# A hybrid decoder layer in split float32: all gate and up panels in rows, on rows that are not normed, with the tokens' factor spread by loads

## The chip, the cores and the metric

The kernel runs on one core of one Trainium2 chip. The metric is the device time of one execution in microseconds (us); the median of several executions counts. TensorE (PE) multiplies matrices into PSUM, VectorE (DVE) and ScalarE (ACT) work elementwise, GpSimd (POOL) does a few small things, and SyncE (SP) issues the DMA transfers. A granted clock of 1.0 is full speed for TensorE.

## The reference

One layer on 256 tokens of width 1024, everything in float32:

```python
h    = rms_norm(x, ln1_g)
proj = h @ w_in                     # q, k, v, z, xbc, dt, gate_a, gate_b
y_a  = moba_attention(norm(q), norm(k), v) @ w_o_attn
y_b  = mamba2_mixer(z, xbc, dt, ...) @ w_o_ssm
x    = x + (sigmoid(gate_a) * y_a + sigmoid(gate_b) * y_b) @ w_out
h2   = rms_norm(x, ln2_g)           # x * rsqrt(mean(x * x) + eps) * ln2_g
g_ff, u_ff = split(h2 @ w_gate_up)  # 1024 x 5632
x    = x + (silu(g_ff) * u_ff) @ w_down
h3   = rms_norm(x, ln3_g)
x    = x + (p @ w_ple_proj) * sigmoid(h3 @ w_ple_gate)
```

An RMS norm is a factor for each token (one over the root of its mean square) times a gain for each feature. The factor of a token can be taken out of a matrix product and applied to the sums; the gain cannot.

## The kernel before

**Split numbers.** Each product is made in parts to keep float32's precision: a number is the sum of a rounded high part and the low rest. For weights the high part `wh` is made by ScalarE, the low part `wl` by VectorE (`split_w`, L257). Of the four products of parts, three are made (high by high, high by low, low by high).

**Weights.** All weights stream from DRAM once. `next_chunk` (L318) loads a chunk of four k-tiles (512 rows) by 512 columns as two tiles of 512 KB, by SP, and splits each. There are five raw buffers, four of `wh` and six of `wl` (L252), so that loads and splits run ahead of TensorE until buffers are short.

**Two forms of a panel.** A panel is 512 columns of a product over all 1024 rows of the weights, in two chunks.
- `Panel` (L334) is over tokens: the activations are the stationary operand, the weights are streamed. For each k-tile and each half of the tokens there are three products of 512 columns. The result has tokens on partitions, so a token's factor is a scale for each partition, but features that go into the next product must be transposed afterwards.
- `Rows` (L379) has the weights stationary and streams the activations' rows, high and low part side by side (2 x 256 columns). For each k-tile and each tile of 128 features there is one product of 512 columns with `wh` and one of 256 with `wl`. The halves of the sums are added afterwards on VectorE. The result has features on partitions, as the next product needs it, and the tokens run along the free axis, so a token's factor would have to be a row of 256 that stands on all partitions.

`Rows.add_all` (L386) makes blocks of two k-tiles for one feature tile (two products with `wh`, two with `wl`). In the first chunk the blocks are sorted by feature tile, in the second by k-tiles. After the last block of a feature tile `after` takes its sums.

**Order of the work.** TensorE's order is written out: the main products follow each other, and a `Filler` (L78) puts small tasks (transposes, the scan's and attention's products) between them once a planned time has come; `LAG` (L68) holds the waiting times, in planned ns. `fill.drain` runs tasks until some condition holds. On the other engines a planner orders instructions by priority: weights ("w") first, then evacuations ("ev"), then background ("bg").

**The tokens' factor, first norm.** `x_stats` (L414) computes `rstd1` with tokens on partitions. `norm_task` (L437) makes a row of it on all partitions: ScalarE scales the identity by it, TensorE multiplies that by a matrix of ones (L444), ScalarE copies the result out twice. Then the eight row tiles are multiplied by it and split.

**The tokens' factor, second norm.** `Residual.take` (L1053) adds the residual, starts the transposes and splits into rows that carry the gain but not the factor (`split_t`, L990), and computes `rstd2`. The first two of the eleven gate and up panels are over tokens (`pair`, L1068), on these rows without the factor; `evac_gu` (L1095) scales the sums by `rstd2`, and `ff_task` (L1105) transposes and splits the result. Beside them `norm2` (L1120) spreads `rstd2` by ones as above (L1130) and makes eight normed rows: high and low part added, multiplied by the factor, split again (L1138 to L1142). The other nine panels are in rows, on the normed rows. For each, `rows_gu` (L1145) copies a feature tile's sums (ScalarE), adds their halves (L1152), and `end` (L1156) makes silu(g) * u, its high and its low part.

Of the kernel before, what the change touches and what calls it, by code (L numbers as in the profile page):

```python
# [36 lines left out]
    ('q', 1, 512),  # L37
    ('k', 0, 1024),
    ('k', 1, 1536),
# [29 lines left out]
    "norm": 0, "norm.x": 7982, "norm.k": 5731, "dt": 3113, "dt.t": 1660, "dt.e": 891, "dt.low": 0,  # L69
    "dt.end": 5490, "xbc": 3857, "xbc.t": 2999, "xbc.end": 16627, "z": 0, "z.t": 3129, "z.end": 768,  # L70
    "qk": 15739, "qk.t": 6258, "qk.end": 0, "v": 1782, "cb": 3077, "rows": 0, "prep": 877, "seg": 102,
    "seg.next": 9127, "out": 8638, "out.xdt": 352, "out.end": 545, "off": 3241, "off.end": 51, "finish": 4321,
    "finish.ones": 8093, "sc": 1152, "sc.tr": 1416, "tr": 2000, "tr.val": 0, "val": 5094, "val.end": 1076,
    "m": 811, "res": 3010, "ff": 0, "ff.end": 500, "n2": 1163, "n2.rows": 2102, "n2.k": 0, "gu": 0,
# [34 lines left out]
def tile_layer(ctx: ExitStack, tc: tile.TileContext, head, xk, pt, vec, w_dt, w_big, w_dn2, w_pp, out):  # L109
# [15 lines left out]
    psb = ctx.enter_context(tc.tile_pool(name="psb", bufs=4, space=bass.MemoryType.PSUM))  # L125
    fill = Filler()
# [69 lines left out]
    with prio("w"):  # L196
        zero = nc.const_aps.tensor(0.0, (P, P), F32)
        pw = pb([512])
        for _ in range(7):
            nc.tensor.matmul(pw[:, :P], zero, zero, start=True, stop=True)  # L200
# [8 lines left out]
        ones_m = const.tile([P, P], F32, name="ones_m")  # L209
        nc.gpsimd.memset(ones_m, 1.0)  # L210
# [168 lines left out]
    class Rows:  # L379
# [6 lines left out]
        def add_all(self, acts, after):  # L386

            for c0 in (0, 4):
                parts = next_chunk()
                runs = [(k0, b) for k0 in (c0, c0 + 2) for b in range(4)]  # L390
                for k0, b in runs if c0 else sorted(runs, key=lambda r: r[1]):
                    cs = slice(b * P, b * P + P)
                    with prio("mm"):
                        for k in (k0, k0 + 1):
                            mm(self.ps[b], parts[k % 4][0][:, cs], acts[k], k == 0, False, main=True)
                        for k in (k0, k0 + 1):
                            mm(self.ps[b][:, :T], parts[k % 4][1][:, cs], acts[k][:, :T], False, k == 7, main=True)
                    fill.now += 52.0
                    fill.step()
                    if k0 == 6:  # L400
                        after(b, self.ps[b])
# [34 lines left out]

    def norm_task():  # L437
        yield fill.now + LAG["norm"]
        with prio("bg"):
            dg = s2([2, P])  # L440
            for tt in range(2):
                act(dg[:, tt], ident, scale=rstd1[:, tt : tt + 1])
            pr = pb([512])
            mm(pr[:, :T], ones_m, dg.rearrange("p a t -> p (a t)"), True, True)  # L444
            rbc = s2([2, T])
            for j in range(2):
                act(rbc[:, j], pr[:, :T])
# [24 lines left out]
    e1d = ctx.enter_context(tc.tile_pool(name="dram", bufs=1, space=bass.MemoryType.DRAM)).tile([32, P], F32, name="e1d")  # L472
# [517 lines left out]
    def split_t(toks, scale_cols, const_scale, acts, delay, tiles=None):  # L990

        th = s4([4, T], F32R)
        tl = s4([4, T], F32R)
        if tiles is not None:
            tiles.append((th, tl))
        yield fill.now + delay
        for jj in range(2):
            with prio("bg"):
# [8 lines left out]
                else:  # L1007
                    for j in range(2):
                        k = 2 * jj + j
                        act(th[:, k], pm[:, j], scale=scale_cols[k])  # L1010
                        stt(tl[:, k], pm[:, j], scale_cols[k], th[:, k].bitcast(F32), op0=ALU.mult, op1=ALU.subtract)
            yield fill.now
        acts.extend((th[:, k], tl[:, k]) for k in range(4))
# [32 lines left out]
    class Residual:  # L1046


        def __init__(self, base, vcol, dst_rstd):
            self.base, self.vcol, self.dst, self.acts, self.tiles = base, vcol, dst_rstd, [[], []], []  # L1050
            self.ss = const.tile([P, 2, 2], F32, name=nm("ss"))

        def take(self, n, pan):  # L1053
# [4 lines left out]
            fill.spawn(split_t([b[:, 0], b[:, 1]], [v[:, self.vcol + 4 * n + k : self.vcol + 4 * n + k + 1] for k in range(4)], None, self.acts[n], LAG["res"], self.tiles), 0)  # L1058
# [21 lines left out]
    res2 = Residual(xin, V_G2, rstd2)  # L1080
# [14 lines left out]
    def evac_gu(_, pan):  # L1095
        t = s2([2, T])
        with prio("ev"):
            for tt in range(2):
                r = rstd2[:, tt : tt + 1]
                act(t[:, tt], pan.ps[tt][:, :T], AF.Sigmoid, scale=r)  # L1100
                stt(t[:, tt], pan.ps[tt][:, :T], r, t[:, tt], op0=ALU.mult, op1=ALU.mult)
                stt(t[:, tt], pan.ps[tt][:, T:], r, t[:, tt], op0=ALU.mult, op1=ALU.mult)
        fill.spawn(ff_task(t), 0, LAG["ff"])

    def ff_task(t):  # L1105
        with prio("bg"):
            pm = pb([2, T])
            for tt in range(2):
                for j in range(2):
                    transpose(pm[:, j, tt * P : tt * P + P], t[:, tt, j * P : j * P + P])  # L1110
            f2 = s4([2, 2, T], F32R)
            fh, fl = f2[:, 0], f2[:, 1]
            act(fh, pm)
            nc.vector.tensor_sub(fl, pm, fh.bitcast(F32))
        yield fill.now + LAG["ff.end"]
        ff.extend((fh[:, j], fl[:, j]) for j in range(2))

    h2n = []

    def norm2():  # L1120

        yield fill.now + LAG["n2"]
        with prio("bg"):
            dg = s2([2, P])
            for tt in range(2):
                act(dg[:, tt], ident, scale=rstd2[:, tt : tt + 1])
        yield fill.now + LAG["n2.rows"]
        with prio("bg"):
            pr = pb([512])
            mm(pr[:, :T], ones_m, dg.rearrange("p a t -> p (a t)"), True, True)  # L1130
            rbc = s2([T])
            act(rbc, pr[:, :T])
        for k in range(0, 8, 2):
            yield fill.now + LAG["n2.k"]
            th, tl = (res2.tiles[k // 4][m][:, k % 4 : k % 4 + 2] for m in range(2))
            with prio("bg"):
                t = s2([2, T])
                nc.vector.tensor_add(t, th.bitcast(F32), tl.bitcast(F32))  # L1138
                nc.vector.tensor_tensor(t, t, rbc.unsqueeze(1).to_broadcast([P, 2, T]), op=ALU.mult)
                h = s4([2, 2, T], F32R)  # L1140
                act(h[:, :, 0], t)
                nc.vector.tensor_sub(h[:, :, 1], t, h[:, :, 0].bitcast(F32))  # L1142
            h2n.extend(h[:, j].rearrange("p a t -> p (a t)") for j in range(2))

    def rows_gu(i):  # L1145
        gu = s4([4, T])

        def after(b, ps):
            with prio("ev"):
                e = s2([512])  # L1150
                act(e, ps)
                nc.vector.tensor_add(gu[:, b], e[:, :T], e[:, T:])  # L1152
            if b == 3:
# [16 lines left out]

    fill.spawn(norm2(), 0)
    pair(res2.acts, evac_gu)
    h2 = res2.acts[0] + res2.acts[1]
    for i in range(2, 2):
        pan = Panel()
        for hf in range(2):
            pan.add(next_chunk(), h2[4 * hf : 4 * hf + 4], last=hf == 1)
        evac_gu(i, pan)
    fill.drain(lambda: len(h2n) == 8)
    for i in range(2, NFF):  # L1180
        Rows().add_all(h2n, rows_gu(i))
# [24 lines left out]
def _layout(i):  # L1206
# [30 lines left out]
    big += [chunks(gu, 512 * n, 4 * g, 4) for g in range(2) for n in range(2)]  # L1237
    for n in range(2, NFF):
# [39 lines left out]
```

## Time and profile before

| what | value |
|---|---|
| median of 3 runs | 584.73 us (584.73 to 586.01) |
| the profiled execution | 585.25 us |
| its span, first to last instruction | 583.5 us |
| TensorE, products: busy | 578.3 us, 99% |
| VectorE, ScalarE, GpSimd: busy | 457.7, 373.1, 47.4 us |
| moved by DMA | 104.97 MB, mean 180 GB/s |
| granted clock of TensorE | 1.000 |
| DMA queue q1: share of 16 engines' span | 52.9% |

The profile is of one execution. A row of the timeline is: start, length, engine, line, operation, out<-in, shape, count of merged instructions; in brackets the idle time before it and what ended it. All matrix products are issued by a helper at L170, the transposes by one at L192, ScalarE's activations by one at L151, so they are told apart by the names of the tiles: `g` are the sums of a panel over tokens, `gr` those of one in rows, `pb` those of a small task, `wh` and `wl` the weights' parts. Matrix products are pipelined and the length of one covers part of the next; the distance of two starts is what one costs.

### The profile page before, as it was taken

What the parts mean: (1) busy time and instruction counts of PE and PEld (TensorE: products, weight loads), DVE (VectorE), ACT (ScalarE), POOL (GpSimd) and SP (SyncE); (2) the same over time, 40 slices, a digit from 0 to 9 for tenths busy, and PEclk for the clock granted to TensorE, in tenths of its full rate; (3) what the DMA queues carried; (4) which work ended last, traced back from release to release, by engine and by line L of the source; (5) the groups of instructions that cost most, each with busy time, mean ns of one, the idle gap of its engine ahead of it and who ended that gap; (6) DMA issues with size and microseconds to landing.
All of it is one profiled execution on the core that took longest, in us unless ns stands there. A gap on an engine that the chain in (4) does not pass through costs nothing.

```text
span 583.5 us, 8612 instructions
## 1 busy us (share of the span) xinstructions
PE 578.3 (99%) x3119; PEld 490.9 (84%) x3119; DVE 457.7 (78%) x745; ACT 373.1 (64%) x582; POOL 47.4 (8%) x44
## 2 busy tenths in 40 slices
PE   9999999999999999999999999999999999999997
PEld 8888888888888888888888888888888888888886
DVE  5686889998998998998898765897777777546464
ACT  7874678676997668666644345766667567535452
POOL 2003100220000311151101000000000000000000
PEclk9999999999999999999999999999999999999999
DMA  8956455476345424435546575555546646565521
GB/s 314 372 188 223 149 182 189 168 194 225 118 154 181 145 79 140 145 111 181 181 144 198 202 258 176 179 181 192 183 163 206 205 153 208 198 202 181 184 71 72
DMA packets 33322, 104.97 MB, mean 180 GB/s; under 512 B 3616, under 2 KB 7040, under 8 KB 33280
## 3 DMA queue, kind: packets, MB, share of 16 engines
q1 hardware_dynamic: 32992, 104.16, 52.9%
q8 instruction: 24, 0.39, 0.3%
q10 hardware_dynamic: 288, 0.26, 0.2%
q14 instruction: 18, 0.15, 0.1%
HBM read 103.28 MB, written 1.06 MB: 179 GB/s over the span
## 4 chain that ended last, share of the span: by engine, by line
PE 99%; DMA 0%; ACT 0%; DVE 0%; issue 0%
PE g L170 52%; PE gr L170 36%; PE pb L170 7%; PE pb L192 3%; DMA x<-in_head 0%; ACT s L151 0%; DVE s L1199 0%; DVE s L1200 0%; ACT wh L151 0%
## 5 line engine op out<-in xcount | busy, mean ns | idle before, releaser
L260 DVE TENSOR_TENSOR wl<-raw,wh 128x1024 fp32r<-128x1024 f32 (+2 forms) x193 | 230.8, 1203 | 90.9 <-ACT wh L151 89.7
L170 PE MATMUL g<-wh,s 128*128 128x512 f32 (+1 forms) x900 | 282.5, 391 | 0.2 <-ACT wh L151 0.2
L151 ACT ACTIVATE wh<-raw 128x1024 fp32r<-128x1024 f32 (+2 forms) x193 | 198.4, 1037 | 131.6 <-PE g L170 81.5
L170 PEld LDWEIGHTS g<-wh,s 128*128 128x128 f32 x900 | 168.8, 189 | 34.7 <-issue 0.5
L170 PE MATMUL gr<-s,wh 128*128 128x512 f32 x608 | 193.5, 399 | 0.0
L170 PE MATMUL g<-wl,s 128*128 128x512 f32 (+1 forms) x450 | 173.3, 387 | 0.0
L170 PEld LDWEIGHTS gr<-s,wl 128*128 128x128 f32 x608 | 114.2, 188 | 26.9
L170 PE MATMUL gr<-s,wl 128*128 128x256 f32 x608 | 119.9, 278 | 0.0
L170 PEld LDWEIGHTS g<-wl,s 128*128 128x128 f32 x450 | 84.4, 188 | 16.4
L170 PEld LDWEIGHTS gr<-s,wh 128*128 128x128 f32 x608 | 93.5, 189 | 1.5 <-issue 0.5
L151 ACT ACTIVATE s<-s 128x512 f32<-128x512 f32 (+2 forms) x49 | 36.6, 747 | 25.4 <-DVE s L1161 15.6
L151 ACT ACTIVATE s<-gr 128x512 f32<-128x512 f32 x76 | 44.3, 592 | 4.2 <-PE gr L170 2.2
L711 POOL TENSOR_SCALAR_AFFINE_SELECT rr<-a_h 128x512 fp32r<-128x512 f32 x16 | 23.8, 1508 | 159.1 <-PE pb L170 118.6
L151 ACT ACTIVATE s<-pb 128x512 f32<-128x512 f32 (+3 forms) x50 | 24.0, 515 | 18.2 <-PE pb L170 12.5
L574 DVE SCALAR_TENSOR_TENSOR s<-s,vecs,s 128x255 f32<-128x255 f32 (+2 forms) x72 | 33.1, 500 | 0.1
L170 PE MATMUL pb<-s,s 128*64 128x128 f32 (+4 forms) x288 | 31.3, 302 | 0.0
L170 PEld LDWEIGHTS pb<-s,s 128*64 128x64 f32 (+1 forms) x288 | 24.7, 154 | 3.9 <-issue 1.2
L192 PE MATMUL pb<-ident,s 128*128 128x128 f32 x170 | 25.0, 273 | 0.0
L406 POOL TENSOR_TENSOR rstd<-tiny,mhalf 128x2 f32<-128x2 f32 x3 | 2.1, 707 | 261.9 <-DVE tiny L405 242.2
L192 PEld LDWEIGHTS pb<-ident,s 128*128 128x128 f32 x170 | 20.3, 141 | 3.0 <-DVE wl L260 0.4
L151 ACT ACTIVATE s<-s,vecs 128x256 f32<-128x256 f32 (+1 forms) x40 | 20.1, 556 | 0.1
L151 ACT ACTIVATE s<-s,tiny,fq 128x128 f32<-128x128 f32 (+1 forms) x32 | 17.1, 537 | 2.0 <-DVE tiny L856 2.0
(146 smaller groups left out, 341.6 us busy)
## 6 DMA issues: line engine op xcount, KB each, us to landing
raw<-in_w_big SPq DMA_DIRECT2D x176, 512.0 KB
raw<-in_head SPq DMA_DIRECT2D x4, 512.0 KB
s<-in_xk SPq DMA_DIRECT2D x4, 512.0 KB
raw<-in_head SPq DMA_DIRECT2D x7, 256.0 KB
e1c<-e1d SPq DMA_DIRECT2D x2, 512.0 KB
raw<-in_w_pp SPq DMA_DIRECT2D x2, 512.0 KB
raw<-in_w_dn SPq DMA_DIRECT2D x2, 512.0 KB
out<-s SPq DMA_DIRECT2D x3, 256.0 KB
```

Source lines behind the costliest of these rows:

```text
L151: return nc.scalar.activation(o, i, f, **kw)
L170: ins = nc.tensor.matmul(o, lhsT, rhs, start=start, stop=stop).ins
L192: queue(nc.tensor.transpose(o, i, ident[: i.shape[0], : i.shape[0]]).ins, False)
L260: nc.vector.tensor_sub(wl, raw, wh.bitcast(F32))
L406: nc.gpsimd.tensor_tensor(dst, t, mhalf[:, : ss.shape[-1]], op=ALU.pow)
L574: stt(cc[:, sft:], u[:, b, : T - sft], cw[3 - sft], cc[:, sft:], op0=ALU.mult, op1=ALU.add)
L711: nc.gpsimd.affine_select(r, bcast(a_h[:, c, h0 : h0 + 4].bitcast(F32), P), pattern=[[0, 4], [1, P]], compare_op=ALU.is_ge, fill=0.0, base ...
```

## The change

- `norm2`, `evac_gu` and `ff_task` go, and with them the two panels over tokens. All eleven gate and up panels are in rows.
- Their rows are those of `split_t`, with the gain and without the factor. `split_t` now writes high and low part of a k-tile side by side, as `Rows` streams them, when it is given a list `rows`.
- The factor is applied behind the sums: `rows_gu` multiplies each added feature tile by `rbc2`, a row of `rstd2` on all partitions.
- That row, and the first norm's, is made by `spread`: SP writes the 2 x 128 factors to DRAM, transposed, and loads them from there onto all partitions. The products with ones, and the matrix of ones, go.
- `Rows.add_all` takes `n`, the k-tiles of a block. Gate and up panels have 4, so the order is four products with `wh`, then four with `wl`, and both chunks run feature tile by feature tile; the others keep 2. Where rows are still being made, it waits for them by chunk.
- Two panels of k change places, and many waiting times in `LAG` are other.

```diff
-    ('k', 0, 1024),
     ('k', 1, 1536),
+    ('k', 0, 1024),
...
-        def add_all(self, acts, after):
+        def add_all(self, acts, after, n=2):
             for c0 in (0, 4):
                 parts = next_chunk()
-                runs = [(k0, b) for k0 in (c0, c0 + 2) for b in range(4)]
+                if len(acts) < 8:
+                    fill.drain(lambda: len(acts) >= c0 + 4)
+                runs = [(k0, b) for k0 in range(c0, c0 + 4, n) for b in range(4)]
...
-                        for k in (k0, k0 + 1):
+                        for k in range(k0, k0 + n):
                             mm(self.ps[b], parts[k % 4][0][:, cs], acts[k], k == 0, False, main=True)
-                        for k in (k0, k0 + 1):
+                        for k in range(k0, k0 + n):
                             mm(self.ps[b][:, :T], parts[k % 4][1][:, cs], acts[k][:, :T], False, k == 7, main=True)
...
+    def spread(dst, col, n):
+        nc.sync.dma_start(rows_d[n].rearrange("t p -> p t"), col)
+        nc.sync.dma_start(dst, rows_d[n : n + 1].rearrange("n t p -> n (t p)").unsqueeze(1).to_broadcast([P] + list(dst.shape[1:])))
+
     def norm_task():
...
-            dg = s2([2, P])
-            for tt in range(2):
-                act(dg[:, tt], ident, scale=rstd1[:, tt : tt + 1])
-            pr = pb([512])
-            mm(pr[:, :T], ones_m, dg.rearrange("p a t -> p (a t)"), True, True)
             rbc = s2([2, T])
-            for j in range(2):
-                act(rbc[:, j], pr[:, :T])
+            spread(rbc, rstd1, 0)
...
-                        act(th[:, k], pm[:, j], scale=scale_cols[k])
-                        stt(tl[:, k], pm[:, j], scale_cols[k], th[:, k].bitcast(F32), op0=ALU.mult, op1=ALU.subtract)
+                        o, ol = (th[:, k], tl[:, k]) if rows is None else (both[jj][:, j, 0], both[jj][:, j, 1])
+                        act(o, pm[:, j], scale=scale_cols[k])
+                        stt(ol, pm[:, j], scale_cols[k], o.bitcast(F32), op0=ALU.mult, op1=ALU.subtract)
...
                 nc.vector.tensor_add(gu[:, b], e[:, :T], e[:, T:])
+                nc.vector.tensor_mul(gu[:, b], gu[:, b], rbc2[:, 0])
...
-    fill.spawn(norm2(), 0)
-    pair(res2.acts, evac_gu)
...
-    for i in range(2, NFF):
-        Rows().add_all(h2n, rows_gu(i))
+    with prio("bg"):
+        rbc2 = s2([1, T])
+        spread(rbc2, rstd2, 1)
+    for i in range(NFF):
+        Rows().add_all(res2.rows, rows_gu(i), 4)
...
-    "m": 811, "res": 3010, "ff": 0, "ff.end": 500, "n2": 1163, "n2.rows": 2102, "n2.k": 0, "gu": 0,
+    "m": 0, "res": 3010, "ff": 8243, "ff.end": 792, "gu": 8000,
```

More of the change, by code (lines that the diff above doesn't have):

```diff
@@ L37 @@
     ('q', 1, 512),
+    ('k', 1, 1536),
     ('k', 0, 1024),
-    ('k', 1, 1536),
     ('gb', 0, 9248),
@@ L68 @@
 LAG = {
[L69 to L73, printed above, removed]
-    "m": 811, "res": 3010, "ff": 0, "ff.end": 500, "n2": 1163, "n2.rows": 2102, "n2.k": 0, "gu": 0,
+    "norm": 2000, "norm.x": 7982, "norm.k": 5429, "dt": 3500, "dt.t": 3631, "dt.e": 4000, "dt.low": 0,
+    "dt.end": 2376, "xbc": 3537, "xbc.t": 3422, "xbc.end": 16627, "z": 12, "z.t": 2127, "z.end": 768,
+    "qk": 15218, "qk.t": 6545, "qk.end": 1000, "v": 0, "cb": 3878, "rows": 145, "prep": 1016, "seg": 184,
+    "seg.next": 7840, "out": 8638, "out.xdt": 527, "out.end": 185, "off": 0, "off.end": 73, "finish": 8000,
+    "finish.ones": 12780, "sc": 1194, "sc.tr": 0, "tr": 1658, "tr.val": 1955, "val": 5094, "val.end": 4010,
+    "m": 0, "res": 3010, "ff": 8243, "ff.end": 792, "gu": 8000,
 }
@@ L125, in tile_layer @@
     psb = ctx.enter_context(tc.tile_pool(name="psb", bufs=4, space=bass.MemoryType.PSUM))
+    dram = ctx.enter_context(tc.tile_pool(name="dram", bufs=1, space=bass.MemoryType.DRAM))
+    rows_d = dram.tile([2, 2, P], F32, name="rows_d")
     fill = Filler()
@@ L208, in tile_layer @@
         nc.gpsimd.memset(m_tmp[:, 0:3], 1.0)
-        ones_m = const.tile([P, P], F32, name="ones_m")
-        nc.gpsimd.memset(ones_m, 1.0)
         nc.gpsimd.affine_select(m_tmp[:, 1], m_tmp[:, 0], pattern=[[-1, P]], compare_op=ALU.is_gt, fill=0.0, base=0, channel_multiplier=1)
@@ L393, in add_all @@
                     with prio("mm"):
-                        for k in (k0, k0 + 1):
+                        for k in range(k0, k0 + n):
                             mm(self.ps[b], parts[k % 4][0][:, cs], acts[k], k == 0, False, main=True)
-                        for k in (k0, k0 + 1):
+                        for k in range(k0, k0 + n):
                             mm(self.ps[b][:, :T], parts[k % 4][1][:, cs], acts[k][:, :T], False, k == 7, main=True)
-                    fill.now += 52.0
+                    fill.now += 26.0 * n
                     fill.step()
-                    if k0 == 6:
+                    if k0 + n == 8:
                         after(b, self.ps[b])
@@ L471, in tile_layer @@
     e1c = const.tile([P, 16, P], F32, name="e1c")
-    e1d = ctx.enter_context(tc.tile_pool(name="dram", bufs=1, space=bass.MemoryType.DRAM)).tile([32, P], F32, name="e1d")
+    e1d = dram.tile([32, P], F32, name="e1d")
     low_h = const.tile([P, P], F32R, name="low_h")
@@ L987, in tile_layer, with split_t @@
         evacuate(kind, i, pan)
[L990 to L995, printed above, removed]
+    def split_t(toks, scale_cols, const_scale, acts, delay, rows=None):
+        if rows is None:
+            th = s4([4, T], F32R)
+            tl = s4([4, T], F32R)
+        else:
+            both = [s4([2, 2, T], F32R) for _ in range(2)]
         yield fill.now + delay
@@ L1009, in split_t @@
                         k = 2 * jj + j
-                        act(th[:, k], pm[:, j], scale=scale_cols[k])
-                        stt(tl[:, k], pm[:, j], scale_cols[k], th[:, k].bitcast(F32), op0=ALU.mult, op1=ALU.subtract)
+                        o, ol = (th[:, k], tl[:, k]) if rows is None else (both[jj][:, j, 0], both[jj][:, j, 1])
+                        act(o, pm[:, j], scale=scale_cols[k])
+                        stt(ol, pm[:, j], scale_cols[k], o.bitcast(F32), op0=ALU.mult, op1=ALU.subtract)
             yield fill.now
-        acts.extend((th[:, k], tl[:, k]) for k in range(4))
+        if rows is None:
+            acts.extend((th[:, k], tl[:, k]) for k in range(4))
+        else:
+            rows.extend(both[k // 2][:, k % 2].rearrange("p a t -> p (a t)") for k in range(4))
     for n in range(2):
@@ L1046, in tile_layer, with __init__ @@
     class Residual:
-        def __init__(self, base, vcol, dst_rstd):
-            self.base, self.vcol, self.dst, self.acts, self.tiles = base, vcol, dst_rstd, [[], []], []
+        def __init__(self, base, vcol, dst_rstd, rows=None):
+            self.base, self.vcol, self.dst, self.acts, self.rows = base, vcol, dst_rstd, [[], []], rows
             self.ss = const.tile([P, 2, 2], F32, name=nm("ss"))
@@ L1057, in take @@
                     nc.vector.tensor_add(b[:, tt], pan.ps[tt], b[:, tt])
-            fill.spawn(split_t([b[:, 0], b[:, 1]], [v[:, self.vcol + 4 * n + k : self.vcol + 4 * n + k + 1] for k in range(4)], None, self.acts[n], LAG["res"], self.tiles), 0)
+            fill.spawn(split_t([b[:, 0], b[:, 1]], [v[:, self.vcol + 4 * n + k : self.vcol + 4 * n + k + 1] for k in range(4)], None, self.acts[n], LAG["res"], self.rows), 0)
             with prio("bg"):
@@ L1079, in tile_layer @@
     rstd3 = const.tile([P, 2], F32, name="rstd3")
-    res2 = Residual(xin, V_G2, rstd2)
+    res2 = Residual(xin, V_G2, rstd2, [])
     pair(m_act, res2.take)
@@ L1093, in tile_layer @@
     ff = []
[L1095 to L1143, printed above, removed]
     def rows_gu(i):
@@ L1169, in rows_gu @@
         return after
-    fill.spawn(norm2(), 0)
-    pair(res2.acts, evac_gu)
[L1173 to L1179, printed above, removed]
-    for i in range(2, NFF):
-        Rows().add_all(h2n, rows_gu(i))
+    with prio("bg"):
[3 more added lines that the diff above has]
+        Rows().add_all(res2.rows, rows_gu(i), 4)
     res3 = Residual(xin, V_G3, rstd3)
@@ L1236, in _layout @@
     big += [chunks(f["w_out"], 512 * n, 4 * g, 4) for g in range(2) for n in range(2)]
-    big += [chunks(gu, 512 * n, 4 * g, 4) for g in range(2) for n in range(2)]
-    for n in range(2, NFF):
+    for n in range(NFF):
         big += [chunks(gu, 512 * n, 4 * g, 4) for g in range(2)]
```

## The prediction

> **What bounds the kernel now.** I read the page first, its busy shares and its chain, and then TensorE's list of waits.
>
> ```profile
> span 583.5 us, 8612 instructions
> ...
> PE 578.3 (99%) x3119; PEld 490.9 (84%) x3119; DVE 457.7 (78%) x745; ACT 373.1 (64%) x582; POOL 47.4 (8%) x44
> ...
> PE 99%; DMA 0%; ACT 0%; DVE 0%; issue 0%
> ```
> ```profile
> PE pb L200 <- PEq L1267: 0.8, 1, 0.8
> PE g L170 <- ACT wh L151: 0.2, 1, 0.2
> ```
>
> The chain that ended last is TensorE for 99% of the span, and the whole list of what TensorE waited for has two entries, 1.0 us together, the first of them at the start. So the time is the sum of TensorE's instructions, each counted from its start to the next one's start (the busy column overlaps neighbours). Work that leaves VectorE or ScalarE gains nothing by itself; work that leaves TensorE gains its full length; and anything new can cost only where it makes TensorE wait. I therefore measured starts on TensorE's timeline.
>
> **The change part by part.** First, the spread of the tokens' factor by a product with ones (L444 and L1130) goes, twice.
>
> ```profile
> 376.16 0.39 PE L170 MATMUL g<-wl,s 128*128 128x512 f32 x1
> 376.63 0.59 PE L170 MATMUL pb<-s,ones_m 128*128 128x256 f32 x2
> 377.29 0.40 PE L170 MATMUL g<-wl,s 128*128 128x512 f32 x1
> ```
> ```profile
> 380.70 0.39 PE L170 MATMUL g<-wl,s 128*128 128x512 f32 x1
> ...
> 393.62 0.39 PE L170 MATMUL g<-wl,s 128*128 128x512 f32 x1
> ```
>
> In a panel over tokens (`Panel`) each block is three products 512 wide (wh, wl, wh), so one `wl` row marks a block. From 380.70 to 393.62 there are 20 such rows, 19 blocks in 12.92 us: 0.680 us a block, 0.227 us a product. Around the ones the step from `wl` to `wl` is 1.13 us instead, so one spread costs 0.45 us of TensorE. Two: **-0.90 us**. ScalarE's scalings of `ident` and its copies go with them, off the path.
>
> Second, the two gate and up panels that ran over tokens had to be transposed afterwards (L1110, four transposes each, in pairs). That goes.
>
> ```profile
> 394.08 0.38 PE L192 MATMUL pb<-ident,s 128*128 128x128 f32 x2
> ...
> 395.84 0.71 PE L170 MATMUL gr<-s,wh 128*128 128x512 f32 x2
> ...
> 396.62 0.38 PE L192 MATMUL pb<-ident,s 128*128 128x128 f32 x2
> 396.76 0.71 PE L170 MATMUL gr<-s,wh 128*128 128x512 f32 x2
> ```
> ```profile
> 399.88 0.62 PE L170 MATMUL gr<-s,wh 128*128 128x512 f32 x2
> 400.34 0.40 PE L170 MATMUL gr<-s,wl 128*128 128x256 f32 x2
> 400.58 0.63 PE L170 MATMUL gr<-s,wh 128*128 128x512 f32 x2
> ...
> 419.39 0.63 PE L170 MATMUL gr<-s,wh 128*128 128x512 f32 x2
> ```
>
> A block of a panel in rows (`Rows`) is two wide products with `wh` and two half-wide ones with `wl`. From 399.88 to 419.39 there are 29 starts, 28 blocks in 19.51 us: 0.697 us each. The block from 395.84 to 396.76 has a pair of transposes in it and takes 0.92 us, so a pair costs 0.22 us, the slow product behind it included. Eight transposes in four pairs: **-0.89 us**.
>
> Third, these two panels become rows. Both forms have 16 blocks a panel (eight k by two token tiles; four pairs of k by four column tiles). Two panels then cost 2 x 16 x (0.697 - 0.680): **+0.54 us**. This is a price, not a gain: the columns streamed are equal, but there are 64 products instead of 48. The Trainium skill ("TensorE: Matmul & The Clock Gate", Back-to-back issue gap) speaks more strongly against rows: it gives a sustained 131 ns a product at 512 columns and 81 ns at 128, so a narrow product costs far more than its share; with 98 ns at 256 (my estimate, on the line between those two) a panel is 48 x 131 = 6.3 us over tokens and 32 x (131 + 98) = 7.3 us in rows, the two panels cost +2.1 us, and the sum below comes to nothing. The trace disagrees, with 227 ns a wide product and about 118 ns a narrow one (0.24 us for the two from 400.34).
>
> Fourth, four k-tiles a block: the sequence wide, wide, narrow, narrow becomes four and four, in all eleven panels. Nothing before shows it. The nearest row is the cut last panel, where narrow products follow each other without a break.
>
> ```profile
> 578.16 0.28 PE L170 MATMUL pb<-wl,s 128*128 128x256 f32 x1
> ...
> 578.88 0.28 PE L170 MATMUL pb<-wl,s 128*128 128x256 f32 x1
> ```
>
> There six products lie between the two rows: 0.120 us each. With wide ones at 0.227 a block should be 2 x 0.227 + 2 x 0.120 = 0.693; measured is 0.697. If that 0.0035 belongs to the changes between wide and narrow, halving them gives 11 x 16 x 0.0018 = 0.3 us. The low end is every product at its share of the 0.680: -176 x 0.017 = -3.0 us. The high end is narrow ones at 0.120 while the wide ones keep the 0.233 of the mixed block (0.46 to 0.47 for two): 1.412 for eight products against 1.394, 88 times, +1.6 us. I take **-0.3 us**, because the long run of narrow products is the same kind of sequence.
>
> Fifth, the spread by loads. The new write to `rows_d` waits on SP for `rstd`, and the read behind it waits for the write; queued behind both are the weight loads.
>
> ```profile
> SPq L545 <- DMA e1d<-e1t: 4.2, 1, 4.2
> SPq L272 <- DVE wl L260: 309.9, 130, 6.4
> ```
> ```profile
> L454 DVE TENSOR_TENSOR xraw<-xraw,s x1: 420/420/420, 33.8 to 33.8; 128x256 f32<-128x256 f32 x1
> ```
> ```profile
> L406 POOL TENSOR_TENSOR rstd<-tiny,mhalf x3: 697/697/727, 24.0 to 559.1; 128x2 f32<-128x2 f32 x3
> ```
> ```profile
> 368.70 0.70 POOL L406 TENSOR_TENSOR rstd<-tiny,mhalf 128x2 f32<-128x2 f32 x1 [52.52 <-DVE tiny L405]
> ```
> ```profile
> 374.64 0.87 DVE L1011 SCALAR_TENSOR_TENSOR s<-pb,vecs,s 128x256 fp32r<-128x256 f32 x2
> ```
>
> The kernel already has one such round trip (`e1d`), and SP stood 4.2 us in it without an entry in TensorE's list. SP's own list says why: in 130 cases it waited for a raw buffer to come free, so loads run as far ahead as five buffers allow, and one holds 12 products over tokens, 2.7 us of TensorE. Cost 0; it becomes a cost when SP is held longer than the four other buffers last, 10.9 us. I price write and read at 4.2 us each, 9 us with their issues. The first spread then lands at 24.0 + 0.7 + 9 = 33.7, where today the first multiplications by the factor run (33.8): no change for the normed rows. For the second, `rstd2` is ready at 368.70 + 0.70 = 369.4, and the factor at about 378.4. The first user is the multiplication on VectorE behind the first sums. The two panels over tokens began at 394.08 - 96 x 0.227 - 0.45 = 371.8; in rows with four k-tiles the first column tile is done 5 blocks of 1.39 us later, 378.8, and copied and added by about 379.8. That is 1.4 us of room; past it, the weight splits queued behind that multiplication wait. The Trainium skill ("DMA: Bandwidth & Descriptors", Anatomy of one DMA) gives a fixed 2.0 us a transfer, by which, with 0.26 MB to read at its 436 GB/s, the estimate for the round trip is 4.6 us and the room nearly 6; "Specifications" there warns that pieces under 512 B are written by read-modify-write, and here they are of 4 bytes. No row before shows a write of this shape.
>
> The rows of the second half (k 4 to 7) are now needed after half a row panel, 371.8 + 5.6 = 377.4, and before after two half panels; their last split ended at 374.64 + 0.87 = 375.5. Cost 0, with 1.9 us of room.
>
> Sixth, VectorE and weights. norm2's twelve operations (L1138 to L1142) go; they cost TensorE nothing. One multiplication per column tile comes, 44 in all.
>
> ```profile
> 440.00:473.00 33.00, 33.00 (x191) 28.78 (x191) 24.00 (x33) 21.65 (x30) 0.00 (x0) 1.00 0.55 188
> ```
> ```profile
> 436.82 1.06 ACT L151 ACTIVATE wh<-raw 128x1024 fp32r<-128x1024 f32 x1 [1.47 <-issue]
> ...
> 439.61 1.06 ACT L151 ACTIVATE wh<-raw 128x1024 fp32r<-128x1024 f32 x1
> ```
> ```profile
> 437.91 1.23 DVE L260 TENSOR_TENSOR wl<-raw,wh 128x1024 fp32r<-128x1024 f32 x1 [1.12 <-ACT wh L151]
> ...
> 444.29 0.69 DVE L1165 TENSOR_TENSOR s<-s,s 128x512 fp32r<-128x512 f32 x1 [0.70 <-ACT s L151]
> ```
>
> VectorE (the third busy number) works 24.00 of 33 us here, 8.1 us of a panel's 11.15; four multiplications at 0.42 (L454 above has their shape) make 9.8, still under 11.15. Cost 0 while splits come in time. With four k-tiles a block both tiles of the second chunk stay in use until its end, so their `wh` buffers (four in all) come free together, and the next panel's second chunk needs both tiles almost at once. Today that chunk's splits start about 2.8 us apart (436.82, 439.61). Afterwards both would start near 439 and be through both engines near 442.4 (2 x 1.06 + 1.23). The row panels began at 394.1 with 0.9 us of transposes among them, so the fifth starts 4 x 11.15 later, at 439.6, and its second chunk at 445.2: 2.8 us of room.
>
> The new waiting times in `LAG` and the swap of the two k panels reorder the same products. Their bounds are -0.2 us (the one wait inside the stream) and +0.8 us (the longest wait in the list); I take 0.
>
> **Sum:** -0.90 - 0.89 + 0.54 - 0.3 = **-1.5 us**; with the bounds of the fourth and last parts, -4.4 to +1.2. The profiled execution took 585.25 us, 1.75 more than its span, and is 0.52 above the median of 584.73. So 583.7 for such an execution, **583.2** on the median.
>
> **The rivals.** (a) *Four k-tiles run at full streaming.* All eleven panels at 0.680 a block: the third term vanishes and nine old panels gain 9 x 0.27 = 2.4, so -1.8 - 2.4 = -4.2 us, 580.5. For it: the wide product at 0.227 elsewhere. Against it: 0.120 in the unbroken narrow run. Half of it is enough to pass 0.3%. (b) *Weight splits come late, in every gate and up panel.* If VectorE's queue puts over 2.8 us (as much as one `end`: three operations of 0.69 and its 0.70 of waiting for ScalarE; an added multiplication is then too much) between a `wh` copy and its `wl`, TensorE waits in each panel. One us past that point costs 11 us: about 593. For it: room falls and VectorE goes from 73% to 88% busy. Against it: splits have the first priority, and `end` is now put 8 us later, behind them. (c) *The gain is eaten:* the second spread lands some 5 us after that estimate, VectorE's splits stand behind it, and TensorE, which has a chunk in hand, waits 1 to 2 us once: 584.2 to 585.2, no change. The Trainium skill's rule on narrow products would end near the same place, through the third term, but nine panels in rows already contradict it; I give it nothing beside (c).
>
> **How the numbers follow.** A measurement of this kernel can tell about 0.3%, 1.75 us. My sum of -1.5 is just inside. The forecast has 0.65; its own range is 582.3 to 584.0, which crosses 582.98, so I count 0.40 of it as no change and 0.25 as faster. (a) 0.15, all faster. (b) 0.13, slower. (c) 0.07, no change. That makes faster 0.40, same 0.47, slower 0.13. For the range I reach most of the way to (a), 581.0, and on the other side past (c) to a small piece of (b), 585.6; left out are about 0.07 below and 0.12 above.
>
> **What would show it.** No product on `ones_m`, eight fewer transposes of `ident`; eight products of a gate and up panel spaced 1.39 us; a panel 11.1 us apart by VectorE's `end` operations; TensorE's list of waits still near 1 us; SP waiting some 4 us twice on `rows_d`; VectorE near 88% in that stage. I am wrong if a wait of `gr` on a `wl` or `wh` appears in each panel, if eight products take 1.36 us, or if the stages ahead of the residual have shifted by more than the one spread.

## The result, and the profile after

The changed kernel takes **591.48 us** (median of 6 runs, 590.33 to 592.62); the kernel before, run beside it, 584.82 (584.73 to 587.96). The ratio is 1.0099 with a 95% interval of 1.0081 to 1.0118: 1% slower, where I forecast 583.2 and a range up to 585.6. The profiled execution has a span of 590.0 us, 6.5 more than before.

The page of the kernel after, with the lines that answer to those shown of before:

```profile
span 590.0 us, 8700 instructions
...
PE 580.6 (98%) x3139; PEld 492.8 (84%) x3139; DVE 464.1 (79%) x781; ACT 370.4 (63%) x577; POOL 44.2 (7%) x43
...
PEclk9997999999999999999999999999999999999999
...
PE 91%; DMA 6%; DVE 1%; SPq 0%; ACT 0%; issue 0%; POOL 0%
PE g L172 42%; PE gr L172 40%; PE pb L172 6%; PE pb L194 3%; DMA s<-in_w_dt 2%; DMA raw<-in_head 2%; DMA rows_d<-rstd 2%; DMA s<-rows_d 1%; DVE wl L260 0%; DVE xraw L452 0%; SPq L421 0%; DVE s L461 0%; SPq L245 0%; POOL rstd L408 0%; ACT wh L153 0%
```

The chain that ended last is no longer TensorE alone. The new transfers, the write `rows_d<-rstd` and the read `s<-rows_d`, stand in it, and the granted clock has one slice at 0.7, the fourth (44 to 59 us). What TensorE waited for:

```profile
PE g L172 <- DVE wl L260: 2.3, 1, 2.3
PE g L172 <- ACT wh L153: 1.9, 3, 1.3
PE pb L202 <- PEq L1217: 0.8, 1, 0.8
```

The list has grown by 4.0 us, all of it waiting for weight splits: 3.5 of it near 45 us, and 0.5 at 6 us, long before the first spread. Where in the kernel the time was lost can be read from GpSimd's `rstd` operations: the second marks the beginning of the gate and up panels, the third the end of what follows them. Before, the second began at 368.70 (shown in the prediction); the third, and then both of the kernel after, on GpSimd's timeline:

```profile
559.08 0.70 POOL L406 TENSOR_TENSOR rstd<-tiny,mhalf 128x2 f32<-128x2 f32 x1 [189.68 <-DVE tiny L405]
```
```profile
375.11 0.70 POOL L408 TENSOR_TENSOR rstd<-tiny,mhalf 128x2 f32<-128x2 f32 x1 [57.47 <-DVE tiny L407]
565.47 0.70 POOL L408 TENSOR_TENSOR rstd<-tiny,mhalf 128x2 f32<-128x2 f32 x1 [189.66 <-DVE tiny L407]
```

The part up to the second `rstd` grew by 6.41 us. From the second to the third it took 190.38 us before and 190.36 after: it gained nothing and lost nothing. So there are two questions: what happened ahead of 375 us, where the change has little more than the first spread, and where the gain of the gate and up panels went.

The chain of waits of the kernel after between 20 and 60 us (start, length, what) answers the first as far as one trace can:

```profile
25.91 9.24 DMA rows_d<-rstd
...
35.16 6.97 DMA s<-rows_d
```

The write took 9.24 us and the read 6.97. The row is there at 42.1; I had reckoned with 33.7. Now VectorE's timeline of the kernel after (in brackets the idle time before the operation and what ended it), and of the kernel before:

```profile
42.16 0.43 DVE L455 TENSOR_TENSOR x<-x,s 128x256 f32<-128x256 f32 x1 [4.83 <-DMA s<-rows_d]
...
46.95 1.21 DVE L260 TENSOR_TENSOR wl<-raw,wh 128x1024 fp32r<-128x1024 f32 x1
```
```profile
40.06 1.22 DVE L260 TENSOR_TENSOR wl<-raw,wh 128x1024 fp32r<-128x1024 f32 x1
```

VectorE stood 4.83 us in front of the first multiplication by the factor. The split that ran at 40.06 before (the twentieth in both kernels) stands behind the multiplications in its order, and runs at 46.95. ScalarE stood in the same way, and its part of that split, `wh`, came at 44.37:

```profile
42.62 0.51 ACT L153 ACTIVATE s<-x 128x256 fp32r<-128x256 f32 x1 [5.97 <-DVE x L455]
...
44.37 1.04 ACT L153 ACTIVATE wh<-raw 128x1024 fp32r<-128x1024 f32 x1
```

TensorE's timeline shows what that cost, and a second loss behind it:

```profile
43.79 0.39 PE L172 MATMUL g<-wh,s 128*128 128x512 f32 x1
45.46 0.51 PE L172 MATMUL g<-wh,s 128*128 128x512 f32 x1 [1.29 <-ACT wh L153]
48.22 0.80 PE L172 MATMUL g<-wl,s 128*128 128x512 f32 x1 [2.25 <-DVE wl L260]
48.82 1.05 PE L172 MATMUL g<-wh,s 128*128 128x512 f32 x2
49.67 0.63 PE L172 MATMUL g<-wl,s 128*128 128x512 f32 x1
```

From 43.79 to 48.82 there are three steps of 0.227 us each at best; they take 5.03, so 4.35 us are lost, nearly all of it in standing (some 0.2 of it is the third step's, at a lower clock already). The two products from 48.82 to 49.67 then take 0.425 us each. The windows view (after the busy times of the five engines: granted clock, DMA share, GB/s) says why:

```profile
46.00:48.00 2.00, 0.00 (x0) 0.00 (x0) 2.00 (x5) 2.00 (x4) 0.00 (x0) 0.66 0.00 0
...
50.00:52.00 2.00, 2.00 (x6) 1.52 (x6) 2.00 (x5) 0.49 (x1) 0.00 (x0) 0.50 0.75 252
...
54.00:56.00 2.00, 2.00 (x10) 1.65 (x9) 0.93 (x3) 1.06 (x1) 1.86 (x1) 1.00 0.90 262
```

The granted clock fell to 0.50 and was back at 1.00 by 54. By TensorE's starts 11 products ran at the low clock, 0.2 us too long each: 2.2 us. Together that is 6.55 us; less the 0.45 that the dropped ones give back, 6.1, against the 6.41 by which this part grew. The 0.5 at 6 us is about what is left. (Profiles of one and the same first part differ by up to 0.5, as runs 1 and 6 below show: 368.08 and 368.62.)

### The profile page after: what moved, and what is told of

Its sections match the earlier page's. It is cut to its first block, busy times and chain, and to the rows that moved or that the text cites. A ratio compares the mean times of both kernels' runs of the same rounds, so it can differ in the third digit from the quotient of the medians.

```text
span 590.0 us, 8700 instructions
## 1 busy us (share of the span) xinstructions
PE 580.6 (98%) x3139; PEld 492.8 (84%) x3139; DVE 464.1 (79%) x781; ACT 370.4 (63%) x577; POOL 44.2 (7%) x43
## 4 chain that ended last, share of the span: by engine, by line
PE 91%; DMA 6%; DVE 1%; SPq 0%; ACT 0%; issue 0%; POOL 0%
PE g L172 42%; PE gr L172 40%; PE pb L172 6%; PE pb L194 3%; DMA s<-in_w_dt 2%; DMA raw<-in_head 2%; DMA rows_d<-rstd 2%; DMA s<-rows_d 1%; DVE wl L260 0%; DVE xraw L452 0%; SPq L421 0%; DVE s L461 0%; SPq L245 0%; POOL rstd L408 0%; ACT wh L153 0%
## 5 line engine op out<-in xcount | busy, mean ns | idle before, releaser
L172 PE MATMUL g<-wh,s 128*128 128x512 f32 (+1 forms) x836 | 263.6, 392 | 1.9 <-ACT wh L153 1.9
L172 PE MATMUL gr<-s,wh 128*128 128x512 f32 x672 | 199.1, 397 | 0.0
L172 PEld LDWEIGHTS g<-wh,s 128*128 128x128 f32 x836 | 157.5, 190 | 34.6 <-ACT wh L153 2.9
L172 PE MATMUL g<-wl,s 128*128 128x512 f32 (+1 forms) x418 | 162.1, 390 | 2.3 <-DVE wl L260 2.3
L172 PEld LDWEIGHTS gr<-s,wh 128*128 128x128 f32 x672 | 110.2, 189 | 9.3 <-issue 0.2
L172 PEld LDWEIGHTS g<-wl,s 128*128 128x128 f32 x418 | 79.0, 190 | 18.4 <-DVE wl L260 2.9
L153 ACT ACTIVATE s<-gr 128x512 f32<-128x512 f32 x84 | 49.5, 594 | 20.9 <-PE gr L172 19.6
L712 POOL TENSOR_SCALAR_AFFINE_SELECT rr<-a_h 128x512 fp32r<-128x512 f32 x16 | 21.1, 1337 | 155.1 <-PE pb L172 114.4
L153 ACT ACTIVATE s<-pb 128x512 f32<-128x512 f32 (+3 forms) x45 | 21.7, 520 | 12.2 <-PE pb L172 9.8
L1109 DVE TENSOR_TENSOR s<-s,s 128x256 f32<-128x256 f32 x44 | 18.5, 420 | 1.1 <-DMA s<-rows_d 0.7
```

The source lines that it names most:

```text
L153: return nc.scalar.activation(o, i, f, **kw)
L172: ins = nc.tensor.matmul(o, lhsT, rhs, start=start, stop=stop).ins
L712: nc.gpsimd.affine_select(r, bcast(a_h[:, c, h0 : h0 + 4].bitcast(F32), P), pattern=[[0, 4], [1, P]], compare_op=ALU.is_ge, fill=0.0, base ...
L1109: nc.vector.tensor_mul(gu[:, b], gu[:, b], rbc2[:, 0])
```

## The experiments

The trace leaves open why the row came so late, and why that stopped TensorE. Three theories, which the expectations call by letters (their rival D is everything else in the change). **A, the order:** the row is late, and VectorE and ScalarE, whose order is fixed, stand in front of it with weight splits behind. **B, SP:** SP stands in the wait between write and read, and the weight loads queued behind it come late. **C, the DMA engines:** the write's 4-byte pieces hold up the engines, so that all transfers come late, weights too.

| kernel | median us (runs) | ratio to before |
|---|---|---|
| 1. after, first spread by ones | 585.16 (10) | 1.0003 [0.9994, 1.0013] |
| 2. before, first spread by loads | 593.04 (4) | 1.0136 [1.0119, 1.0153] |
| 3. after, uses asked for later | 599.30 (4) | 1.0250 [1.0235, 1.0265] |
| 4. after, spreads on GpSimd's queue | 590.07 (4) | 1.0086 [1.0071, 1.0101] |
| 5. by ones, and the write alone | 585.27 (10) | 1.0001 [0.9992, 1.0010] |
| 6. by ones, two k-tiles a block | 584.00 (11) | 0.9981 [0.9973, 0.9990] |
| 7. after, factors written in rows | 584.66 (11) | 0.9994 [0.9985, 1.0002] |
| 8. after, uses behind two splits | 587.42 (4) | 1.0044 [1.0028, 1.0059] |
| 9. in rows, two k-tiles a block | 584.14 (12) | 0.9982 [0.9972, 0.9992] |
| 10. by ones, write of 8-byte pieces | 584.95 (1) | a single run |
| 11. by ones, write of pieces apart | 585.19 (1) | a single run |

**1. The first spread by a product again.** The kernel after, with the old way for `rstd1` alone.

```diff
...
+            pr = pb([512])
+            mm(pr[:, :T], ones_m, dg.rearrange("p a t -> p (a t)"), True, True)
             rbc = s2([2, T])
-            spread(rbc, rstd1, 0)
+            for j in range(2):
+                act(rbc[:, j], pr[:, :T])
```

> The changed kernel with the first spread made by the product with ones again, all else as changed. In the changed kernel's trace TensorE stands for 4.3 us between 43.8 and 48.8 us and then runs eleven products at 0.427 us instead of 0.227 (2.2 us). Theory A (the first factor's row lands at 42.1, VectorE and ScalarE stand in front of its uses, weight splits are queued behind them), B (SP stands in its wait for the write, weight loads are queued behind it) and C (the write of 4-byte pieces slows the DMA engines) all expect the 6.6 us gone: 584.8, within 0.7 of the kernel before, because gate and up panels came out at no gain. Rival D (the new waiting times or the four k-tiles cost the time) expects 590 or more.

585.16 us: against the kernel after, 6.3 us are gone. All of the loss belongs to the first spread, and the second one, which this kernel keeps, does no harm.

**2. The other way round: before, with nothing but the first spread by loads.**

```diff
...
-            mm(pr[:, :T], ones_m, dg.rearrange("p a t -> p (a t)"), True, True)
...
+            spread(rbc, rstd1, 0)
```

> The kernel before with the first spread by loads, nothing else. A, B and C: TensorE waits near 45 us here too, about 6 us slower than before, 591. D: half a microsecond faster than before, 584.4.

593.04 us, 7.9 above before. No other part of the change is needed for the loss, which is 1.6 larger here than in the kernel after. TensorE's list of waits and ScalarE's timeline of this kernel:

```profile
PE g L172 <- ACT s L153: 6.1, 1, 6.1
```
```profile
43.07 0.51 ACT L153 ACTIVATE s<-x 128x256 fp32r<-128x256 f32 x1 [3.90 <-DVE x L455]
43.49 1.25 ACT L153 ACTIVATE s<-g,rstd 128x512 f32<-128x512 f32 x2
```

TensorE does not wait for weights near 45 us here. ScalarE stands in front of the late rows, and behind them in its order is the evacuation of a panel (`s<-g,rstd`), so TensorE waits for PSUM. The row is late as there (VectorE stands 5.05 us for it, until 42.61), the victim another: whatever stands behind it in a fixed order.

**3. The uses asked for later.** A longer planned pause between the spread and the multiplications.

```diff
-    "norm": 2000, "norm.x": 7982, "norm.k": 5429, ...
+    "norm": 2000, "norm.x": 2500, "norm.k": 1500, ...
...
             spread(rbc, rstd1, 0)
+            yield fill.now + 11000
```

> The changed kernel with 11 planned us between the first spread and its uses, so that weight splits come ahead of them on VectorE and ScalarE; SP's order keeps its wait. A: no wait of TensorE near 45 us, 584.4. B and C: the loads behind SP's wait are still 3 us late and still slow, TensorE still waits 2 us or more and loses its clock: 588 or more.

A miss. VectorE's first multiplication still ran ahead of the splits (at 41.87, after 5.17 us of standing), so the edit did not do what it was made for: the planner, I suppose, pulled it forward. And with the rest of the norm moved in the plan, new waits came later. The longest of them in TensorE's list:

```profile
PE pb L172 <- DVE a_l L528: 3.8, 1, 3.8
```

It says nothing for or against A, except that a planned time is not an order. Run 8 does it properly.

**4. Both spreads issued by GpSimd**, so that SP never waits for them.

```diff
-        nc.sync.dma_start(rows_d[n].rearrange("t p -> p t"), col)
+        nc.gpsimd.dma_start(rows_d[n].rearrange("t p -> p t"), col)
```

(and the read likewise)

> The changed kernel with both loads of each spread issued by GpSimd, on a queue of their own; SP has no wait for them, the write is the same. A: if the row lands before 37 us, where VectorE last worked in time, no wait, 584.4; every us later is about one us of wait. B: the wait goes wherever the row lands, 584.4. C: the weights' packets still take over 2 us each behind the write, TensorE still waits: 587 or more.

590.07 us. SP issued five weight loads from 26.34 on without standing at `rows_d`, and yet the write took longer, by the list of DMA issues (last column: us from issue to landing), and TensorE waited as before:

```profile
rows_d<-rstd POOLq DMA_DIRECT2D x1, 1.0 KB, 10.9
```
```profile
PE g L172 <- DVE wl L260: 3.4, 1, 3.4
```

B falls as the cause: without SP's standing, all but 1.4 us of the loss is still there.

**5. The write alone.** Run 1's kernel, with the 4-byte write added where it stood. Nothing reads it.

```diff
+            nc.sync.dma_start(rows_d[0].rearrange("t p -> p t"), rstd1)
```

> The first spread by the product with ones as in e1, and beside it the write of the 2 x 128 factors to DRAM in 4-byte pieces, which nobody waits for and nobody reads. If the write by itself slows the DMA engines (C), weight packets between about 27 and 36 us take over 2 us each here too, and the loads issued before and during it land some 5 to 8 us late. C as the sole cause: TensorE waits 3 us or more near 45, 590. A (the late landing of the row in front of VectorE's and ScalarE's queues does it): the packets are slow, but TensorE does not wait, 585.2 within 0.7.

585.27 us, the same as without it. But the write slows the transfers just as in the kernel after. The windows view (the last two columns: DMA share, GB/s) of before, of after and of this kernel:

```profile
30.00:32.00 2.00, 2.00 (x11) 1.65 (x10) 1.53 (x2) 1.07 (x1) 0.00 (x0) 1.00 0.60 174
32.00:34.00 2.00, 2.00 (x10) 1.66 (x9) 0.97 (x3) 0.94 (x3) 0.00 (x0) 1.00 0.84 260
```
```profile
32.00:34.00 2.00, 2.00 (x10) 1.69 (x9) 1.06 (x2) 1.06 (x1) 0.00 (x0) 1.00 0.63 21
```
```profile
30.00:32.00 2.00, 2.00 (x10) 1.67 (x9) 1.70 (x3) 1.49 (x2) 0.00 (x0) 1.00 0.71 16
32.00:34.00 2.00, 2.00 (x10) 1.66 (x10) 0.94 (x1) 0.00 (x0) 0.00 (x0) 1.00 0.64 16
```

Before, the engines moved 260 GB/s in the latter window; with the write they are nearly as busy (0.63 to 0.71 against 0.84), and move 16 to 21. In windows of 1 us, run 5 stays at 61 GB/s or less from 29 to 37 us. C is right that the engines are held up, and wrong that this by itself costs: weights late by that much are still in time when no late row stands in front of their splits.

**6. Two k-tiles a block** in the gate and up panels of run 1's kernel, for the second question.

```diff
-        Rows().add_all(res2.rows, rows_gu(i), 4)
+        Rows().add_all(res2.rows, rows_gu(i), 2)
```

> e1 with two k-tiles a block in the gate and up panels instead of four. In the changed kernel eight products take 1.403 us there, in the kernel before 1.394: over 88 groups of eight 0.8 us, so 584.4 against e1's 585.2. My prediction's term (four k-tiles gain 0.3) would have it 0.3 slower than e1.

584.00 us, 1.2 below run 1. GpSimd's timeline of run 1, then of this kernel:

```profile
368.08 0.70 POOL L410 TENSOR_TENSOR rstd<-tiny,mhalf 128x2 f32<-128x2 f32 x1 [57.46 <-DVE tiny L409]
558.45 0.70 POOL L410 TENSOR_TENSOR rstd<-tiny,mhalf 128x2 f32<-128x2 f32 x1 [189.67 <-DVE tiny L409]
```
```profile
368.62 0.70 POOL L410 TENSOR_TENSOR rstd<-tiny,mhalf 128x2 f32<-128x2 f32 x1 [57.46 <-DVE tiny L409]
558.09 0.70 POOL L410 TENSOR_TENSOR rstd<-tiny,mhalf 128x2 f32<-128x2 f32 x1 [188.77 <-DVE tiny L409]
```

Between the two `rstd` lie 190.37 us with four k-tiles and 189.47 with two. Four k-tiles cost 0.90 us, and that is where the stage's gain went: with two, it is 0.91 us shorter than before.

**7. The factors written in rows.** TensorE transposes the two columns of factors, ScalarE copies the two rows of 128, and SP writes two pieces of 512 bytes in place of 256 of 4. All else is as in the kernel after.

```diff
-        nc.sync.dma_start(rows_d[n].rearrange("t p -> p t"), col)
+        pc = pb([P])
+        transpose(pc[:2], col)
+        act(rows_s[:2, n], pc[:2])
+        nc.sync.dma_start(rows_d[n], rows_s[:2, n])
```

(`rows_s` is a new tile in SBUF)

> The changed kernel with only the form of the write changed, for both spreads: TensorE transposes the 128 x 2 factors (one small transpose), ScalarE copies two rows of 128, and SP writes them in two pieces of 512 bytes. SP's waits, the load and the place of the uses ahead of the next weight split stay. If 4-byte pieces are what makes write and engines slow (C as the first link): write done in 5 us or less, row there by 35, no wait of TensorE near 45, 584.5. If any write and load of this kind is late there (the queues are full of weights): row still past 40 and 588 or more.

584.66 us: 6.8 less than after, and TensorE's list has 0.2 us beside the entry at the start. SP's and VectorE's timelines, and the window that stood at 21 GB/s:

```profile
28.54 0.31 SPq L445 DMA_DIRECT2D rows_d<-rows_s  x1
29.10 1.98 SPq L273 DMA_DIRECT2D raw<-in_w_big  x2
31.13 0.43 SPq L446 DMA_DIRECT2D s<-rows_d  x1
```
```profile
38.87 0.43 DVE L459 TENSOR_TENSOR x<-x,s 128x256 f32<-128x256 f32 x1 [2.27 <-DMA s<-rows_d]
```
```profile
32.00:34.00 2.00, 2.00 (x11) 1.65 (x10) 0.51 (x2) 1.06 (x1) 0.00 (x0) 1.00 0.72 252
```

The write is done within 2.6 us of its issue (28.54 to 31.13; in the kernel after 9.24, part of which may be the weight loads in front of it: it was issued 2.6 us earlier, while the engines still moved some 400 GB/s). The read still takes 7.7 us until VectorE goes on, behind two weight loads in the same queue, so the row is there later than the 35 that I expected. The multiplications begin at 38.87, 5 us later than before, and TensorE does not notice; 3.3 us later still, in the kernel after, it does.

**8. The uses behind the next two splits**, by an order given to VectorE, and not by a time.

```diff
...
-                    nc.vector.tensor_mul(xraw[k // 2], xraw[k // 2], rbc)
+                    follow(nc.vector.tensor_mul(xraw[k // 2], xraw[k // 2], rbc).ins, last_wl[0])
...
```

(`last_wl` is the last split so far; a pause of 27000 planned ns lets two more be issued, with `norm.x` and `norm.k` shortened to 3600 and 3000)

> The changed kernel with the first uses of the loaded row put behind the next two weight splits on VectorE and ScalarE by an explicit order (e3 had not moved them). Write, load and SP's waits as in the changed kernel, so the row still lands near 42. A: those splits run by about 41, no wait of TensorE near 45, 584.8 (up to 1 more if normed rows come late for the panel of gate b). B and C alone: the wait stays, 588 or more.

VectorE's timeline and TensorE's list:

```profile
39.21 2.55 DVE L261 TENSOR_TENSOR wl<-raw,wh 128x1024 fp32r<-128x1024 f32 x2 [1.14 <-ACT wh L153]
41.82 0.42 DVE L457 TENSOR_TENSOR x<-x,s 128x256 f32<-128x256 f32 x1
```
```profile
PE g L172 <- DVE s L463: 0.7, 2, 0.4
```

The write is the same, SP stands as long, and the read is issued at 34.96, as late as in the kernel after (35.16); VectorE takes the row at 41.82. With the splits ahead of the multiplications the wait near 45 us is gone, and so is the low clock. A is shown. The time itself lies between the two that I had named: 587.42 us is 4 below the kernel after, yet 2.8 above run 7, and that is only in part accounted for: the normed rows themselves now come late for later panels (0.7 us in the list; the profiled execution, 586.22, was the shortest of its four, and what the others lost I did not trace).

**9. Rows, and two k-tiles a block:** runs 6 and 7 together.

> e7 (both factors written in two pieces of 512 bytes) with two k-tiles a block. If e6's gain of 1.1 over e1 belongs to the blocks and e7's 0.5 to the two small transposes in place of a product with ones, they add: 583.6, and the fastest of the kernels here. If four k-tiles helped anywhere, 584.7 or more.

584.14 us, ratio 0.9982: with run 6 the best version, about 1 us below the kernel before. That is within what I called no change, and half a microsecond above what I expected of the two together.

**10 and 11. What about the write is slow.** Run 5 again, with the unread write in other shapes: 128 pieces of 8 bytes in one run of 1 KB, and 256 pieces of 4 bytes with addresses 512 bytes apart.

```diff
-            nc.sync.dma_start(rows_d[0].rearrange("t p -> p t"), rstd1)
+            nc.sync.dma_start(rows_d[0].rearrange("t p -> (t p)").rearrange("(p t) -> p t", t=2), rstd1)
```
```diff
-            nc.sync.dma_start(rows_d[0].rearrange("t p -> p t"), rstd1)
+            nc.sync.dma_start(apart_d[:, :, 0], rstd1)
```

> e5 with its lone write turned: each partition writes its two factors as one piece of 8 bytes, all 128 pieces in one run of 1 KB. If the pieces' size (small against 512 bytes) is what slows the engines, weight packets over 2 us and the write done some 9 us after its issue as in e5. If the scattering of two 4-byte pieces a partition does it, a write done in 4 us and no slow packets.

> e5 with its lone write spread out: the 256 pieces of 4 bytes go to addresses 512 bytes apart, so that no two share a line of memory. If small pieces as such slow the engines, as in e5. If many pieces meeting in the same 1 KB of DRAM do it, no packets over 2 us and a write done in about 4 us.

The windows of both, in this order:

```profile
30.00:32.00 2.00, 2.00 (x10) 1.65 (x10) 2.00 (x2) 1.06 (x1) 0.00 (x0) 1.00 0.44 18
32.00:34.00 2.00, 2.00 (x11) 1.66 (x10) 0.76 (x2) 1.46 (x3) 0.00 (x0) 1.00 0.93 367
```
```profile
30.00:32.00 2.00, 2.00 (x10) 1.66 (x9) 1.98 (x2) 1.00 (x1) 0.00 (x0) 1.00 0.61 186
32.00:34.00 2.00, 2.00 (x10) 1.69 (x9) 0.50 (x2) 1.33 (x3) 0.00 (x0) 1.00 0.96 330
```

Half as many pieces, twice as large and close together, hold the engines up for about half as long: in windows of 1 us they stay at 41 GB/s or less from 28 to 32 us, and then are back at 367. As many pieces as in run 5, as small, but 512 bytes apart, do not hold them up at all (186 and 330; before 174 and 260). So it isn't the size or the number of pieces alone; small pieces side by side in memory are what is slow, as far as one execution of each shows.

## Why the prediction was wrong, point by point

**The step that failed** is the fifth: "I price write and read at 4.2 us each ... The first spread then lands at ... 33.7 ...: no change for the normed rows." Three things in it were wrong. The price of the write came from the `e1d` round trip, which writes 32 rows of 512 bytes; this write has 256 pieces of 4 bytes, and took 9.24 us, with pieces of 512 bytes under 2.6. Second, the price of the read was too low as well: it took 6.97 us. Of the 8.4 us between 33.7 and 42.1, 4.7 are the write's and 2.5 the read's (each had 4.5, its issue included), and 1.2 come from a later start (25.91 in place of 24.7). I quoted the rule that bears on the write. The Trainium skill ("DMA: Bandwidth & Descriptors", Specifications) says that below 512 bytes a transfer does read-modify-write. Runs 5 and 7 agree in direction; run 11 does not, as its pieces are just as small and hold nothing up. What matters is that pieces lie close together, and that they hold up the other transfers too (16 to 21 GB/s in place of 260). The 2.0 us that I took from the same page of the Trainium skill ("Anatomy of one DMA") stands there for transfers that GpSimd issues; run 4, where GpSimd issued the write behind weight loads, had 10.9. Third, I asked what is queued behind the late row only for the second spread, where I counted 1.4 us of room. At the first, the sum left 0.1 us of room (33.7 against 33.8), the same fixed order held splits behind the row, and I gave lateness there no price.

**Rival (c)** had the mechanism (VectorE's splits stand behind a late row), but at the second spread and for 1 to 2 us. There SP issued the write at 375.84 and the read at 383.44, again late, and VectorE's timeline shows how little was left of it:

```profile
387.68 0.42 DVE L1109 TENSOR_TENSOR s<-s,s 128x256 f32<-128x256 f32 x1 [0.73 <-DMA s<-rows_d]
```

0.73 us of VectorE, and none of TensorE. What I had left out altogether is that a wait of TensorE is paid again in its clock: a stop that lost 4.35 us cost 2.2 more.

**The fourth term had the wrong sign.** Predicted -0.3 us, measured +0.90 (run 1 to run 6). TensorE's timeline of the kernel after:

```profile
378.24 1.09 PE L172 MATMUL gr<-s,wh 128*128 128x512 f32 x4
379.17 0.64 PE L172 MATMUL gr<-s,wl 128*128 128x256 f32 x4
379.64 1.09 PE L172 MATMUL gr<-s,wh 128*128 128x512 f32 x4
...
383.85 1.09 PE L172 MATMUL gr<-s,wh 128*128 128x512 f32 x4
```

Four blocks of eight take 5.61 us, 1.4025 each, where twice the block of four was 1.394: 88 times 0.0085 is +0.75 of the 0.90; the rest I did not trace. The four narrow products take 0.47, 0.1175 each, about what I had assumed. But the four wide ones take 0.93, 0.2325 each: they keep the pace of the mixed block and do not fall to the 0.227 of a panel over tokens. That is what the high end that I gave (1.412) assumed of the wide ones; what I took for a cost of changing between wide and narrow was not one.

**What was right.** Without four k-tiles the stage between the two `rstd` is 0.91 us shorter than before; the sum of its terms, one spread (-0.45), eight transposes (-0.89) and two panels as rows (+0.54), was -0.80. Run 9, with both spreads by loads in a form that does no harm, is 1.05 us below before (0.5 to 1.6 by the interval), and the three terms give -1.25. Rival (b) did not come (and eleven panels at 1 us each on top of 583.2 would be 594, not 593): VectorE works 27.90 of 33 us, 85% (I had said 88), and TensorE waits for nothing there.

```profile
440.00:473.00 33.00, 33.00 (x190) 28.80 (x189) 27.90 (x45) 21.00 (x31) 0.00 (x0) 1.00 0.56 182
```

SP's stand did no harm by itself, as I had said: run 8 has it, and TensorE waits for no split there; run 4 has none, and is only 1.4 us better off. For the span, -1.5 was forecast and +6.5 measured: of the 8.0 between them, 6.9 is the first spread (the 6.41, and the 0.45 that it was to give), 1.2 the k-tiles, and the other terms gave 0.1 back.

## What to carry to other kernels

Before a product is replaced by a trip through DRAM, look at the shape of the write: a column that becomes a row is one piece for each element, and a few such bytes can hold up every transfer for some 8 us (run 5). Then look, at each place where the result is used, at what stands behind that use in its engine's fixed order; a late operand costs nothing by itself, and everything once a weight split or a PSUM evacuation is behind it. Where TensorE is the bound, a wait of several microseconds is paid again in part through its clock, here half as much again.

## What the runs showed of the hardware

- A write of 256 neighbouring pieces of 4 bytes took 9.24 us (10.9 on GpSimd's queue), and the 16 DMA engines together fell to some 20 GB/s meanwhile; 128 pieces of 8 bytes held them up about half as long (4 us against 8); 256 pieces 512 bytes apart held nothing up; 2 pieces of 512 bytes were written in under 2.6 us. Why neighbours are slow no run shows.
- The clock after a stop. In the kernel after TensorE stood twice, 1.29 and 2.25 us by its timeline, with a single product between, and then ran at 0.50 until about 53 us. The Trainium skill ("TensorE: Matmul & The Clock Gate", What's actually happening) says that the clock is halved after an idle window of about 3.4 us and released after about as much work; the traces agree in part. The granted clock is 0.50 there, and it stayed low for 3.4 us in run 4 (46.9 to 50.3) and for twice that, 6.8, in the kernel after (46.6 to 53.4) and in run 2 (43.0 to 49.8). But in the kernel after it fell only some 2.4 us after TensorE first stood, with a product in between, so a stop shorter than 3.4 us was enough, and 11 products of 0.425 us ran before it was back.
- A wide product costs 0.227 us in a panel over tokens and 0.2325 in a panel in rows, also behind another wide one. No run was made on the reason.
